# Scheduling the splits behind a rotation, and the split of the recurrence's input, behind the products traced ahead of them

## The chip, the cores and the metric

The kernel runs on one core of a Trainium2 chip. The metric is the device time of one execution in microseconds (us). Before the change it is 1851.07 us, the median of three runs (1850.51 to 1853.98). The execution that the profiler recorded took 1852.94 us; its span, from the first to the last instruction, is 1851.2 us, and 1.7 us lie around it.

## The reference

Two layers of a hybrid block on x of 512 tokens x 1024, all in fp32. Cut to what matters here:

```python
h = rms_norm(x, g_pre_mix);  proj = h @ w_in      # q k v qi ki wi xr gr zu zv gates
q, k, qi, ki = (apply_partial_rope(t) for t in (q, k, qi, ki))   # the rotation
score = einsum(wi, relu(qi . ki)) * idx_scale      # the indexer: 8 heads
sel = top_k(score, 128)                            # keys that each query may see
y_a = softmax(q . k on sel) @ v                    # 8 heads of attention
xr = causal_depthwise_conv(xr)
y_b = rg_lru(xr) * gelu(gr)                        # the recurrence
y_c = gelu(zu) * spatial_gating(rms_norm(gelu(zv)))
x = x + rms_norm((sum_n sigmoid(gate_n) * (y_n @ w_branch_n)) @ w_out)
x = x + rms_norm(relu(rms_norm(x) @ w_up)**2 @ w_dn)
x = x + rms_norm((p @ w_ple) * sigmoid(x @ w_gate))
```

## The kernel before, in words

Activations lie transposed in SBUF, 128 features by 512 tokens to a tile. To keep fp32 accuracy, each operand of a product is split in two fp32r halves, hi (a cast on ACT) and lo (a subtraction of hi, on DVE or POOL), and a product is three matmuls on PE: hi.hi, lo.hi, hi.lo (`mm3`, lines 298 to 300).

**Weights.** They come in tiles of 128x1024 in the order written out in `order`. `prep` (line 231) does one: a DMA on SP's queue into one of 3 buffers `wr`, the cast `wh` on ACT (line 243), the subtraction `wl` on DVE (line 244). There are 4 buffers for `wh` and `wl`, so the preparation of a tile waits until PE has finished the tile four places earlier. `getw` (line 247) fetches a tile and prepares up to three ahead. A tile of `w_in` is 24 matmuls of 512 columns (`proj`, through `gemm`).

**The order of the work.** A Python program traces the instructions; a planner in the framework then fixes, once and on estimated durations, the order of each engine's queue: of the instructions whose inputs it holds for ready it takes the one traced first. On the chip each engine takes its queue in that order. The trace itself is ordered by a clock of its own, `clk`: each step of a product advances it by its length in us (`tick`), and `defer(us, fn)` has `fn` traced when the clock has come that much further. `run_later(force=True)` traces all that is left at once. Generators (the indexer, attention, the recurrence) are advanced in the same way.

**The beginning of a layer.** `xr0` to `xr3` are projected while x arrives (`gemm_arriving`), in two halves of 256 tokens in the second layer; the norm's factors R come from `Stats.row`, whose `complete` defers a few small instructions (`rstd_tok`: products on PE at line 408, DVE at 427, POOL at 428; then a transposition on PE at 434 and a copy on ACT at 443). Then the convolution for `xr` on DVE (606 to 611), then `ki`, `qi0` to `qi3`. `rope` (line 570) is the rotation: DVE multiplies and shuffles the product (573, 574), POOL multiplies and adds (575, 576). Its result is split for the next products by `ki_split` (ACT 369, 628, 629, DVE 370), `stacked` (ACT 650 twice, DVE 651 twice) or `q_split` (ACT 1026 and 1028, DVE 1027), deferred by TURN = 5. `xc_split` (ACT 616, POOL 617) splits the convolution's output; only the recurrence's gates use it, much later. `wi_turn` transposes the indexer's weights on PE (639).

**Then** `tokens(1, ...)` (line 580) projects zv: four weight tiles ("chunks") for two token blocks at a time, 12 matmuls to a chunk in each of two passes (line 590), zu, the spatial gating, gr, the recurrence, and the gates and branches. The indexer (products at 667 to 671 or 681, scores on ACT 692 and DVE 695 to 699, then 96 rounds of max and replace on DVE at 714 and 716 in both layers) runs as a generator beside all of these and gives the mask BIAS (POOL 729, 730). It is forced to its end by `finish(idxq)` after the first q and k of attention. In attention, `logits` wait for Q and K; the softmax is DVE 939 and 941, ACT 940 and 942; `turn` transposes on PE (953) and splits on ACT 369 and DVE 370; `values` are products at 967.

Of the kernel before, what the change touches and what calls it, by code (L numbers as in the profile page):

```python
# [17 lines left out]
S = 512  # L18
# [27 lines left out]
def f32v(ap):  # L46
    return ap.bitcast(F32)
# [3 lines left out]
def hybrid_block_kernel(ctx, tc, xT, pT, pos, vec, bsp, freq, w_in, w_tok, w_lru, w_sp, w_br, w_out, w_up, w_dn, w_ple, w_gate, out, depth=DEPTH, dbg=None):  # L51
    nc = tc.nc
# [14 lines left out]
    def tmp(dt=F32):  # L67
        return tp.tile([128, S], dt, tag="tmp", name=nm("tmp"), bufs=NTMP)
# [4 lines left out]
    def bank():  # L73
        return pp.tile([128, 512], F32, tag="ps", name=nm("ps"), bufs=8)

    def slot(tag, dt=F32, big=False):
        return cp.tile([128, 4, S] if big else [128, S], dt, tag=tag, name=nm(tag))
# [10 lines left out]
    TAIL = 3  # L88
    LEAD = 256
    ATT = 13  # L90
    TURN = 5
    WARM = 120
    FIRST = [0, 1, 4]

# [152 lines left out]
    def getw(key, ahead=LA):  # L247
        assert order[nget[0]][0] == key, (order[nget[0]][0], key)
        nget[0] += 1
        while nprep[0] < min(nget[0] + ahead, len(order)):  # L250
            prep()
        return prepared.pop(key)
# [8 lines left out]
    def defer(us, fn):  # L261
        later.append((clk[0] + us, uid[0], fn))
        uid[0] += 1

    def run_later(force=False):
        while later:
            later.sort(key=lambda e: e[:2])
            if not force and later[0][0] > clk[0]:
                return
            later.pop(0)[2]()  # L270

    def add_task(q, gen):
        q["wait"].append(gen)
# [17 lines left out]
    def finish(q):  # L291
        run_later(force=True)
        while q["act"] or q["wait"]:
            tick(0.3)
# [7 lines left out]
    def gemm(ps, w, xs, kk, c0=0, st=None, r=FULL):  # L302

        h3, l3 = [v.rearrange("p (k c) -> p k c", k=kk) for v in w]
        for k in range(kk):
            if st is not None and k == kk - 2:
                st.partial()
            mm3(ps, h3[:, k, c0:c0 + 128], l3[:, k, c0:c0 + 128], xs[k][0][:, r], xs[k][1][:, r], k == 0, k == kk - 1)
            tick(0.65 * width(r) / S)
# [67 lines left out]
    class Stats:  # L377
# [59 lines left out]
        def row(self, div, dst):  # L437


            def complete(r):  # L440
                def tok():
                    self.rstd_tok(div, r)
                    defer(3.0, lambda: A.copy(dst[:, r], self.rstd_bc(r)))

                defer(2.2, tok)

            return complete

# [84 lines left out]
    for l in range(depth):  # L533
        vc = vecs[l]

        def col(c):
            return vc[:, c:c + 1]
# [18 lines left out]
        def proj(name, ahead=LA):  # L556
            ps = bank()
            gemm(ps, getw(("in", l, name), ahead), XS, KT)
            return ps
# [11 lines left out]
        def rope(ps, n=128):  # L571
            t1, u = tmp(), tmp()
            V.tensor_mul(t1[:n], ps[:n], Cr[:n])
            V.stream_shuffle(u[:n], ps[:n], mask=SHUF)
            G.tensor_mul(u[:n], u[:n], Sr[:n])  # L575
            G.tensor_add(t1[:n], t1[:n], u[:n])  # L576
            return t1
# [19 lines left out]
        idxq = {"wait": [], "act": [], "max": 1}  # L597
# [5 lines left out]
        for j in range(4):  # L603
            ps = first[j]
            xr = tmp()
            V.tensor_mul(xr, ps, R)
            xc = slot(f"M{4 + j}")
            A.activation(xc, xr, AF.Identity, bias=col(V_CB + j), scale=col(V_CW + 12 + j))
            for i in range(3):
                s = 3 - i  # L610
                V.scalar_tensor_tensor(xc[:, s:], xr[:, :S - s], col(V_CW + 4 * i + j), xc[:, s:], op0=ALU.mult, op1=ALU.add)
            xh, xl = slot(f"B{j}", F32R), slot(f"B{4 + j}", F32R)
            XC.append((xc, xh, xl))

            def xc_split(xc=xc, xh=xh, xl=xl):
                A.copy(xh, xc)
                G.tensor_sub(xl, xc, f32v(xh))

            defer(10 + 5 * j, xc_split)


        ps = proj("ki")
# [5 lines left out]
            A.copy(kih[64:128], kf[0:64])  # L628
            A.copy(kil[64:128], f32v(kil[0:64]))

        defer(TURN, ki_split)
        wf = tmp()
        A.copy(wf, ps)
        WI = small(32, "wi", 2).rearrange("p (t h) -> p t h", t=4)
# [5 lines left out]
            for t in range(1, 4):  # L640
                V.tensor_scalar(WI[:, t, :], pw[:, t * 128 + 64:t * 128 + 72], rt[:, t:t + 1], IDX_SCALE, op0=ALU.mult, op1=ALU.mult)

        defer(9, wi_turn)

        def stacked(f, q0, q1):


            for s, q in enumerate((q0, q1)):
                r, other = slice(64 * s, 64 * s + 64), slice(64 - 64 * s, 128 - 64 * s)
                A.copy(q[r], f[r])  # L650
                V.tensor_sub(q[other], f[r], f32v(q[r]))
            return q0, q1

        QI = []
        for j in range(4):
            ps = proj(f"qi{j}")
            QI.append((slot(f"A{j}", F32R), slot(f"A{4 + j}", F32R)))
            defer(TURN, lambda f=rope(ps), q=QI[j]: stacked(f, *q))

        def qk(a, b, c, d, jobs):  # L660

# [23 lines left out]
        def scores(t, sc):  # L685
            n = 128 * (t + 1)
            qs = slice(t * 128, (t + 1) * 128)
            for j in range(4):
                pr = qk_full(QI[j], kih, kil, t, n)
                for s in range(2):  # L690
                    rl = tmp()
                    A.activation(rl[:, :n], pr[s][:, :n], AF.Relu)
                    w = WI[:, t, 2 * j + s:2 * j + s + 1]
                    if j == 0 and s == 0:
                        V.tensor_scalar(sc[:, :n], rl[:, :n], w, None, op0=ALU.mult)
                    else:
                        V.scalar_tensor_tensor(sc[:, :n], rl[:, :n], w, sc[:, :n], op0=ALU.mult, op1=ALU.add)
                yield 3.4
            V.tensor_add(sc[:, qs], sc[:, qs], tri)

        def indexer():
            sc = {t: tmp() for t in (1, 2, 3)}
            for t in (1, 2, 3):
                yield from scores(t, sc[t])
            for t in (1, 2, 3):
                yield from select(t, sc[t])

        def select(t, sc):
            n = 128 * (t + 1)
            wk = tmp()  # L710
            m8 = None
            for r in range(TOPK // 8):
                m8 = small(8, "m8", 4)
                V.max(m8, (sc if r == 0 else wk)[:, :n])  # L714
                if r < TOPK // 8 - 1:
                    V.match_replace(wk[:, :n], m8, (sc if r == 0 else wk)[:, :n], -3.0e38)  # L716
                yield 0.8 + 1.1 * t
            thr = m8[:, 7:8]
            gt, cnt = tmp(), small(1, "cnt", 4)
            V.tensor_scalar(gt[:, :n], sc[:, :n], thr, None, op0=ALU.is_gt, op1=ALU.add, accum_out=cnt)  # L720
            rem = small(1, "cnt", 4)
            V.tensor_scalar(rem, cnt, -1.0, float(TOPK), op0=ALU.mult, op1=ALU.add)
            eq = tmp()
            V.tensor_scalar(eq[:, :n], sc[:, :n], thr, None, op0=ALU.is_equal)

            V.tensor_tensor_scan(wk[:, :n], eq[:, :n], eq[:, :n], 0.0, ALU.add, ALU.max)
            yield 2.0
            V.scalar_tensor_tensor(eq[:, :n], wk[:, :n], rem, eq[:, :n], op0=ALU.is_le, op1=ALU.mult)
            G.tensor_add(gt[:, :n], gt[:, :n], eq[:, :n])
            G.tensor_scalar(BIAS[t], gt[:, :n], -NEG, NEG, op0=ALU.mult, op1=ALU.add)  # L730
            yield 1.0

        defer(9, lambda: add_task(idxq, indexer()))


        bs = tmp()
# [23 lines left out]
        for j in range(4):  # L760
            ps = proj(f"zu{j}")
# [16 lines left out]
        for j in range(4):  # L778
# [3 lines left out]
            for hf in range(2):  # L782
                ps = bank()
# [4 lines left out]
                for s in range(2):  # L788
                    r = slice(64 * s, 64 * s + 64)
# [55 lines left out]
        for j in range(4):  # L845
# [7 lines left out]
            r, i = tmp(), tmp()  # L853
# [59 lines left out]
        KK = [slot("K0", F32R, True), slot("K1", F32R, True)]  # L913
# [105 lines left out]
        for j in range(4):  # L1019
            f = rope(proj(f"q{j}"))  # L1020
            q2, ql = (slot(f"A{j}", F32R), slot(f"A{4 + j}", F32R)), tmp(F32R)

            def q_split(f=f, q2=q2, ql=ql):
                for s in range(2):
                    r, other = slice(64 * s, 64 * s + 64), slice(64 - 64 * s, 128 - 64 * s)
                    A.copy(q2[s][r], f[r])
                    V.tensor_sub(ql[r], f[r], f32v(q2[s][r]))
                    A.copy(q2[s][other], f32v(q2[s][r]))

            defer(TURN, q_split)  # L1030
            Q.append((q2, ql))
            defer(TURN, lambda f=rope(proj(f"k{j}")), j=j: stacked(f, KK[0][:, j], KK[1][:, j]))
            if j == 0:
                finish(idxq)
            defer(ATT, lambda j=j: add_task(attq, attention(j)))
            gated(1, YB, ds=range(2 * j, 2 * j + 2))
# [23 lines left out]
        for d in range(5):  # L1060
            ps = bank()
# [8 lines left out]
        ps = bank()  # L1070
# [52 lines left out]
        for c in range(2):  # L1123
# [3 lines left out]
            for i in range(4):  # L1127
                ps = bank()
# [14 lines left out]
        for d in range(5):  # L1143
            if d < 4:
                ps = first[d]
            else:
                ps = bank()
# [95 lines left out]
```

## Time and profile before

| | |
|---|---|
| median of three runs | 1851.07 us (1850.51 to 1853.98) |
| the profiled execution | 1852.94 us |
| its span | 1851.2 us, 22873 instructions |
| PE busy | 1803.0 us (97%) |
| DVE busy | 1159.5 us (63%) |
| ACT busy | 800.3 us (43%) |
| POOL busy | 361.6 us (20%) |
| mean granted clock of TensorE | 0.990 |
| chain that ended last | PE 72%, DVE 12%, POOL 6%, issue 6%, ACT 4% |

A busy share says how long an engine had work in it, not that it ran at its peak. PE is busy almost throughout, so what can be won without fewer products is the idle time of PE, some 48 us, and the time in which its clock was granted at less than full. The view of waits says for each of these idle times which instruction ended it.

### The profile page before, as it was taken

The page shows a single profiled execution, that of the slowest core. Times are in us where ns is not written, and L with a number is a line of the kernel's source. Part 1 is how long each engine was busy: PE and PEld are TensorE (multiplying, and loading weights), DVE is VectorE, ACT ScalarE, POOL GpSimd, SP SyncE. Part 2 cuts the span into 40 slices and gives each one's busy share as a digit, 9 for nine tenths or more (in the row PEclk, how much of TensorE's full clock was granted, in tenths as well). Part 3 has the DMA queues.
Part 4 walks back from the last instruction along what each step waited for, and adds up shares of the span by engine and source line. Part 5 has one row for each costly group of instructions (what it writes and reads, how often), then busy time and mean ns, then how long its engine had stood idle before and what let it go on. Part 6 is the DMA issues. An engine that isn't in the chain of part 4 may idle for free.

```text
span 1851.2 us, 22873 instructions
## 1 busy us (share of the span) xinstructions
PE 1803.0 (97%) x8798; PEld 1507.5 (81%) x8798; DVE 1159.5 (63%) x1939; ACT 800.3 (43%) x1292; POOL 361.6 (20%) x292
## 2 busy tenths in 40 slices
PE   8899999999999999999998999999999999999997
PEld 7787887888888888888887878877888888888886
DVE  6689996666386253533685999866563852544355
ACT  5466435664453322223455573455544432222233
POOL 3513212210240000003454141222004200000033
PEclk9999999999999999999999999999999999999999
DMA  5122322222223232332212223222222222222321
GB/s 173 63 92 85 98 92 91 69 80 82 90 80 108 97 98 96 99 106 91 92 58 97 68 92 103 91 80 72 89 80 92 92 92 101 96 97 97 108 80 58
DMA packets 49678, 167.77 MB, mean 91 GB/s; under 512 B 6048, under 2 KB 8864, under 8 KB 49568
## 3 DMA queue, kind: packets, MB, share of 16 engines
q1 hardware_dynamic: 47376, 163.64, 26.8%
q10 hardware_dynamic: 2192, 2.67, 0.4%
q8 instruction: 69, 1.13, 0.3%
q14 instruction: 41, 0.34, 0.1%
HBM read 164.19 MB, written 2.10 MB: 90 GB/s over the span
## 4 chain that ended last, share of the span: by engine, by line
PE 72%; DVE 12%; POOL 6%; issue 6%; ACT 4%; DMA 0%; SPq 0%; POOLq 0%; DVEq 0%; ACTq 0%
PE ps L298 21%; PE ps L299 20%; PE ps L300 20%; PE ps L356 3%; PE ps L590 3%; DVE wl L244 2%; POOL tmp L575 1%; POOL tmp L576 1%; DVE tmp L716 1%; DVE m L714 1%; POOL sacc L398 1%; POOL X L483 1%; PE ps L681 1%; PE ps L967 1%; DVE tmp L790 1%
## 5 line engine op out<-in xcount | busy, mean ns | idle before, releaser
L243 ACT CAST wh<-wr 128x1024 fp32r<-128x1024 f32 x303 | 316.6, 1049 | 453.3 <-PE ps L300 365.9
L244 DVE TENSOR_TENSOR wl<-wr,wh 128x1024 fp32r<-128x1024 f32 x303 | 386.8, 1280 | 188.7 <-ACT wh L243 188.0
L298 PE MATMUL ps<-xh,wh 128*128 128x512 f32 (+1 forms) x1296 | 502.7, 388 | 0.9 <-DVE tmp L370 0.9
L299 PE MATMUL ps<-xh,wl 128*128 128x512 f32 (+1 forms) x1296 | 495.5, 382 | 3.0 <-DVE wl L244 3.0
L300 PE MATMUL ps<-xl,wh 128*128 128x512 f32 (+1 forms) x1296 | 495.6, 382 | 0.0
L398 POOL TENSOR_TENSOR sacc<-sacc,tmp 128x256 f32<-128x256 f32 (+1 forms) x99 | 109.8, 1109 | 894.8 <-issue 584.5
L300 PEld LDWEIGHTS ps<-xl,wh 128*128 128x128 f32 x1296 | 243.9, 188 | 48.2
L299 PEld LDWEIGHTS ps<-xh,wl 128*128 128x128 f32 x1296 | 244.4, 189 | 47.1 <-DVE wl L244 3.9
L298 PEld LDWEIGHTS ps<-xh,wh 128*128 128x128 f32 x1296 | 244.0, 188 | 47.2 <-issue 1.9
L300 PE MATMUL ps<-V,wh 128*128 128x512 f32 (+1 forms) x528 | 195.4, 370 | 0.0
L298 PE MATMUL ps<-K,wh 128*128 128x512 f32 (+1 forms) x432 | 158.2, 366 | 0.0
L299 PE MATMUL ps<-K,wl 128*128 128x512 f32 (+1 forms) x432 | 157.8, 365 | 0.0
L300 PE MATMUL ps<-B,wh 128*128 128x512 f32 x336 | 130.9, 390 | 0.0
L298 PE MATMUL ps<-A,wh 128*128 128x512 f32 x320 | 125.0, 391 | 0.2 <-ACT A L369 0.2
L299 PE MATMUL ps<-A,wl 128*128 128x512 f32 x320 | 124.6, 389 | 0.0
L1102 DVE TENSOR_TENSOR M<-M,ps 128x512 f32<-128x512 f32 x48 | 33.0, 688 | 141.4 <-PE ps L300 141.4
L300 PEld LDWEIGHTS ps<-V,wh 128*128 128x128 f32 x528 | 99.5, 188 | 16.7
L1090 DVE TENSOR_TENSOR tmp<-ps,R 128x512 f32<-128x512 f32 x64 | 43.8, 690 | 108.6 <-PE ps L300 108.5
L356 PE MATMUL ps<-xl,wh 128*128 128x256 f32 (+1 forms) x264 | 88.1, 334 | 6.2 <-DVE xl L503 5.5
L298 PEld LDWEIGHTS ps<-K,wh 128*128 128x128 f32 x432 | 81.5, 189 | 13.3
L299 PEld LDWEIGHTS ps<-K,wl 128*128 128x128 f32 x432 | 81.5, 189 | 13.1
L356 PE MATMUL ps<-xh,wh 128*128 128x256 f32 (+1 forms) x264 | 87.1, 330 | 2.2 <-ACT xh L493 2.2
(237 smaller groups left out, 2733.0 us busy)
## 6 DMA issues: line engine op xcount, KB each, us to landing
wr<-in_w_in_dram SPq DMA_DIRECT2D x95, 512.0 KB, 3.3
wr<-in_w_up_dram SPq DMA_DIRECT2D x64, 512.0 KB, 3.3
wr<-in_w_dn_dram SPq DMA_DIRECT2D x64, 512.0 KB, 3.3
wr<-in_w_br_dram SPq DMA_DIRECT2D x24, 512.0 KB, 3.3
wr<-in_w_tok_dram SPq DMA_DIRECT2D x16, 512.0 KB, 3.3
wr<-in_w_out_dram SPq DMA_DIRECT2D x16, 512.0 KB, 3.3
wr<-in_w_gate_dram SPq DMA_DIRECT2D x16, 512.0 KB, 3.3
X<-in_xT_dram SPq DMA_DIRECT2D x8, 256.0 KB, 5.9
```

Of the source, the lines that this page charges most:

```text
L243: A.copy(hi, raw)
L244: V.tensor_sub(lo, raw, f32v(hi))
L298: PE.matmul(ps, wh, xh, start=start, stop=False)
L299: PE.matmul(ps, wl, xh, start=False, stop=False)
L300: PE.matmul(ps, wh, xl, start=False, stop=stop)
L356: PE.matmul(pss[o][:, r], (h3, l3, h3)[m][:, q], xs[q][m // 2][:, r], start=q == 0 and m == 0, stop=q == KT - 1 and m == 2)
L398: G.tensor_add(sacc[:, r], sacc[:, r], self.q[r.start, r.stop])
L483: (G if d in on_g else V).tensor_add(X[d][:, r], X[d][:, r], ys[d][:, r])
L575: G.tensor_mul(u[:n], u[:n], Sr[:n])
L590: PE.matmul(ps, x, w, start=k == 0 and i == 0, stop=k == KT - 1 and i == 2)
L1090: V.tensor_mul(t, ps, R)
L1102: V.tensor_add(F[d], F[d], ps)
```

## The change

A helper `behind_products(fn)` traces what `fn` traces, and gives each of its instructions on ACT, DVE and POOL an edge to the last PE instruction traced so far. The edge is for the planner alone (no semaphore, nothing on the chip): it may not place the instruction before that product. `turn_later` defers such a call. The splits after a rotation and `xc_split` go through it. TURN goes from 5 to 7, `xc_split` from 10 + 5j to 12 + 5j, `wi_turn` from 9 to 14, the indexer's start from 9 to 12. In `Stats.row`, the first half's `tok` is deferred by 8.0 in place of 2.2; where there are no halves, and for the second half, it stays at 2.2.

```diff
-    TURN = 5
+    TURN = 7
+    def behind_products(fn):
+        ins = nc.cur_bb.bb.instructions
+        n0 = len(ins)
+        mark = next(i for i in reversed(ins[:n0]) if i.engine == mybir.EngineType.PE)
+        fn()
+        for i in nc.cur_bb.bb.instructions[n0:]:
+            if i.engine in (mybir.EngineType.Activation, mybir.EngineType.DVE, mybir.EngineType.Pool):
+                tc.add_manual_dep(i, mark.name, mybir.DependencyInfo(mybir.DependencyClass.NoSync, mybir.DependencyReason.SCHED_ONLY), reason="behind products")
+    def turn_later(us, fn):
+        defer(us, lambda: behind_products(fn))
...
-                defer(2.2, tok)
+                defer(2.2 if r.stop == S else 8.0, tok)
...
-            defer(10 + 5 * j, xc_split)
+            turn_later(12 + 5 * j, xc_split)
...
-        defer(TURN, ki_split)
+        turn_later(TURN, ki_split)
...
-        defer(9, wi_turn)
+        defer(14, wi_turn)
...
-            defer(TURN, lambda f=rope(ps), q=QI[j]: stacked(f, *q))
+            turn_later(TURN, lambda f=rope(ps), q=QI[j]: stacked(f, *q))
...
-        defer(9, lambda: add_task(idxq, indexer()))
+        defer(12, lambda: add_task(idxq, indexer()))
...
-            defer(TURN, q_split)
+            turn_later(TURN, q_split)
...
-            defer(TURN, lambda f=rope(proj(f"k{j}")), j=j: stacked(f, KK[0][:, j], KK[1][:, j]))
+            turn_later(TURN, lambda f=rope(proj(f"k{j}")), j=j: stacked(f, KK[0][:, j], KK[1][:, j]))
```

## Rows read from the trace of the kernel before

**Rows 1.** Waits of PE, whole execution: who <- whom: us in total, times, longest.
```profile
PE ps L590 <- DVE wl L244: 10.5, 4, 4.2
...
PE ps L299 <- DVE wl L244: 4.4, 4, 1.5
PE ps L967 <- ACT tmp L369: 4.1, 4, 2.3
PE ps L434 <- POOL rt L428: 2.5, 3, 1.7
...
PE ps L967 <- DVE tmp L370: 1.7, 4, 0.9
...
PE ps L639 <- ACT tmp L633: 1.2, 2, 0.7
```

**Rows 2.** Stretches: length, busy us (x instructions) PE PEld DVE ACT POOL, clock, DMA.
```profile
75.25:79.46 4.21, 0.00 (x1) 0.01 (x1) 3.98 (x4) 2.50 (x5) 2.27 (x2) 0.74 0.04 17
79.46:83.90 4.44, 4.44 (x11) 3.51 (x12) 3.79 (x6) 0.50 (x1) 1.61 (x1) 0.50 0.49 161
...
994.18:998.60 4.42, 4.42 (x10) 3.46 (x11) 3.80 (x6) 0.50 (x1) 1.58 (x1) 0.50 0.56 170
...
540.00:900.00 360.00, 360.00 (x1600) 298.05 (x1599) 174.35 (x210) 111.19 (x139) 21.05 (x14) 1.00 0.30 99
```

**Rows 3.** ACT in order of time: start, us, instruction [idle before <- releaser].
```profile
60.70 0.62 ACT L369 CAST M<-tmp 64x512 fp32r<-64x512 f32 x1 [5.60 <-POOL tmp L576]
...
63.28 1.06 ACT L243 CAST wh<-wr 128x1024 fp32r<-128x1024 f32 x1
68.21 1.26 ACT L650 CAST A<-tmp 64x512 fp32r<-64x512 f32 x2 [3.87 <-POOL tmp L576]
69.49 1.05 ACT L243 CAST wh<-wr 128x1024 fp32r<-128x1024 f32 x1
74.73 1.26 ACT L650 CAST A<-tmp 64x512 fp32r<-64x512 f32 x2 [4.18 <-POOL tmp L576]
```

**Rows 4.** DVE in order of time, the same stretch.
```profile
70.96 1.23 DVE L244 TENSOR_TENSOR wl<-wr,wh 128x1024 fp32r<-128x1024 f32 x1
...
75.38 2.76 DVE L651 TENSOR_TENSOR A<-tmp,A 64x512 fp32r<-64x512 f32 x2 [1.93 <-ACT A L650]
78.18 1.23 DVE L244 TENSOR_TENSOR wl<-wr,wh 128x1024 fp32r<-128x1024 f32 x1
```

**Rows 5.** POOL in order of time, the same stretch.
```profile
53.95 4.11 POOL L617 TENSOR_TENSOR B<-M,B 128x512 fp32r<-128x512 f32 x1 [1.34 <-ACT B L616]
...
65.53 1.29 POOL L575 TENSOR_TENSOR tmp<-tmp,tmp 128x512 f32<-128x512 f32 x1
...
71.00 2.33 POOL L575 TENSOR_TENSOR tmp<-tmp,tmp 128x512 f32<-128x512 f32 x1 [2.83 <-DVE tmp L574]
```

**Rows 6.** Line 650, whole execution: ACT's idle time before it (us, times) until:
```profile
  POOL tmp L576: 58.6, 16
```

**Rows 7.** Attention of the second layer: ACT in order of time.
```profile
1209.32 1.26 ACT L1026 CAST A<-tmp 64x512 fp32r<-64x512 f32 x2 [5.73 <-POOL tmp L576]
...
1211.76 0.47 ACT L369 CAST tmp<-ps 128x384 fp32r<-128x384 f32 x1
```

**Rows 8.** The same place as a stretch, columns as in Rows 2.
```profile
1212.28:1217.40 5.12, 4.97 (x17) 3.99 (x18) 4.87 (x8) 1.51 (x2) 0.63 (x1) 0.67 0.19 53
```

**Rows 9.** A stretch of the gates and branches, columns as in Rows 2.
```profile
200.00:220.00 20.00, 19.34 (x86) 15.69 (x85) 19.73 (x35) 6.16 (x9) 1.29 (x1) 1.00 0.33 106
```

**Rows 10.** DVE in order of time, just after that stretch.
```profile
219.49 1.21 DVE L244 TENSOR_TENSOR wl<-wr,wh 128x1024 fp32r<-128x1024 f32 x1
```

**Rows 11.** PE in order of time, the first use of that tile.
```profile
221.13 0.39 PE L299 MATMUL ps<-xh,wl 128*128 128x512 f32 x1
```

**Rows 12.** The first softmax of the first layer: ACT, in order of time.
```profile
287.21 0.72 ACT L942 ACTIVATE tmp<-tmp,mx 128x512 f32<-128x512 f32 x1
```

**Rows 13.** PE in order of time, the transposition that reads it.
```profile
287.82 0.60 PE L953 MATMUL ps<-ident,tmp 128*128 128x128 f32 x4
```

## The prediction, made before the changed kernel ran

> **What bounds the kernel now.** I read the waits of PE first, since PE is busy 97% of the span and only its idle time and its clock can be won here. The reader is to see in them that the longest wait which is no start-up of a stage is that of the zv projection (line 590) for a `wl` that DVE makes: 10.5 us in four times, up to 4.2 at once [rows 1]. Then I took stretches around it: from 75.25 to 79.46 PE does nothing at all, and for the next 4.44 us its granted clock is 0.50, the lower level (1.2 GHz), so the wait is paid a second time [rows 2]. The second layer shows the same behind its own wait, 994.18 to 998.60 [rows 2].
>
> Why is that `wl` late? ACT and DVE in order of time answer it. DVE makes the subtraction at 78.18 right behind two of line 651, which had waited for line 650 on ACT [rows 4], and ACT had stood 4.18 us until POOL's rotation was done; the casts of weights at 63.28 and 69.49 likewise come right behind splits that had kept ACT idle for 5.60 and 3.87 us [rows 3]. So an engine with little to do (ACT is idle in most of these rows) is held at the head of its queue by a split whose input POOL has not finished, and the weight behind it, whose raw data and buffer are there, is late. Over the execution ACT lost 58.6 us in 16 such places before line 650 alone [rows 6]. In attention it is the same with line 1026: 5.73 us idle, and only after it the cast (line 369) for which PE's `values` stand 2.3 us [rows 1, 7].
>
> **The change, part by part.** No instruction is added or removed: the edges are for the planner, so there is no new semaphore and no new wait; queues are reordered. I cost each part by the wait it can end. The unit of PE: 1600 matmuls in 360 us, 0.225 each [rows 2], so 12 products of a chunk take 2.7 us and a tile of 24 takes 5.4.
>
> A, *the splits of ki and qi, and `xc_split`, in the zv projection.* Each projection advances the trace's clock by 5.2 (8 steps of 0.65). With TURN = 5 a split was traced in the last step of the next projection, just ahead of the `getw` that prepares a weight; with 7 and the edge it comes some 2 us into the projection after that, so the planner has the cast (1.05) and the subtraction (1.23) of the weight ahead of it [rows 3, 4]: 2.3 us against 2 us and the split's own cast of 0.6. The weights of chunks 1 to 4 so stand in front of the splits that held them. What goes: 10.5 us of waits [rows 1] and the slow clock behind two of them. In 79.46 to 83.90 PE starts 11 products in 4.44 us, for which 2.5 would do: 1.9 lost; in 994.18 to 998.60 it starts 10 in 4.42: 2.2 lost [rows 2]. Together 14.6 us. What is late next: the fourth chunk. Its cast stands behind the second `stacked`, whose rotation POOL finishes only after the two ahead of it and `xc_split`s of up to 4.11 us [rows 5]; a rest of 0.5 us a layer seems likely to me. Bounds: 0 (the weights stay late) to 14.6; I take 13.6, near the upper end, because the rows show no other cause of this wait. `xc_split`, 0.6 on ACT and 4.11 on POOL at worst [rows 5], has only the recurrence's gates waiting for it, some 70 us on; moving it back also lets POOL begin ki's rotation earlier. The DMAs of weights on SP's queue wait for `wr` buffers that `wl` frees, so they move earlier; those of the gating's bias, on ACT's queue, change places with splits and are read after zv.
>
> B, *`wi_turn` from 9 to 14.* PE's transpositions waited 1.2 us in two times for a copy on ACT [rows 1], itself behind `xc_split`s. Five us later the copy is done. 0 to 1.2; I take 1.2. Its three small DVE operations are needed by the indexer only, which starts later still.
>
> C, *the splits of q and k in attention.* The waits of `values` are 4.1 and 1.7 [rows 1]; behind the longest the mean clock is 0.67 over 5.12 us [rows 8], that is 3.4 us at half clock, 1.7 lost. Together 7.5. The split of q(j+1) was traced 5 after its projection, and the planner put it ahead of `turn`'s cast, which [rows 7] then waited for the rotation. Two us later and behind the products it should come after that cast in most rounds. Against it: `logits` of the next round need these splits, and come 13 after k; instead of 8, 6 us are left for 2.7 us of ACT and DVE work. Bounds: -3 (that margin is missed by 0.4 us in each of 8 rounds) to 7.5; I take 5.5, as waits on DVE (1.7) have other work of DVE ahead of them.
>
> D, *the first half's row, 2.2 to 8.0.* Of three waits of line 434 for `rt`, 2.5 us, the one of 1.7 belongs to the last norm, which is not touched [rows 1]; 0.8 is left, in the up projections. The step moves behind the last products of the second half; PE then meets the last `xl` instead, so I take half, 0.4 (0 to 0.8). R as a whole is complete only with its second half, which stays.
>
> E, *the indexer from 9 to 12.* It starts 3 us later against PE's work. In the stretch of gates DVE is busy 19.73 of 20 us [rows 9], so the mask comes up to 3 us later. That costs nothing while the first softmax of attention is ahead of PE; it just is: the last normalisation ends where the transposition of it begins, 287.9 [rows 12, 13]. On the other hand q's split no longer holds DVE there. Bounds 0 to 6 for both layers; I take 1.0.
>
> Sum: 13.6 + 1.2 + 5.5 + 0.4 - 1.0 = 19.7 us. The profiled execution took 1852.94, so 1833.2 for one like it; the median of the runs is 1.9 lower, and from it the forecast is 1831.4 us.
>
> *A rule against it.* POOL's multiplication of a rotation took 1.29 us alone and 2.33 where DVE's `wl` subtraction began beside it [rows 4, 5]. Suppose all POOL work from ki's rotation on met such a subtraction: three rotations of 2 x 2.33 and two `xc_split`s of 4.11 are 22.2 us; from 53.95, where POOL is seen to take up an `xc_split` [rows 5], that is 76.2, and with split, cast and subtraction (1.26, 1.05, 1.23) the fourth chunk is ready at 79.7. The third was wanted at 75.25 after an earlier wait of (10.5 - 2 x 4.2) / 2 = 1.05 [rows 1, 2], so the fourth would be at 74.2 + 2.7 = 76.9. That is 2.8 us of wait and some 2 for the clock behind it, 9.6 in both layers: 10.1 us of gain are left, 1841. The Trainium skill (SBUF — State Buffer, "Who interferes with whom") says that a VectorE instruction with two SBUF inputs and a GpSimd instruction that reads SBUF exclude one another for as long as the first of them lasts. By that rule such meetings are certain once the subtractions stand closer to the rotations; the trace agrees in the pair above (2.33 against 1.29). I keep it a rival, since 1.29 stands in the rows too and not every operation can meet one.
>
> **The rivals.** (1) *Given back to DVE.* In the gates DVE is full [rows 9], and a tile's subtraction ended at 220.70, 0.43 us ahead of its first use [rows 10, 11]; four waits of 4.4 us are there already [rows 1]. If PE comes 7 us earlier and DVE cannot, A is lost again in small waits: 1851.1 - 1.2 - 5.5 - 0.4 + 1.0 = 1845.0. Against it: DVE stood idle in the zv stretch for the same splits [rows 4], and moves forward with PE. (2) *POOL's rotation stays the bound*, as worked out above: 1841. (3) *Not what it says.* The estimated order comes out as before, because on the planner's durations POOL was never late; then only B and D are left: 1851.1 - 1.6 = 1849.5. For it speaks that the old order, too, was made by that planner; against it that the edge bars the old place. (4) *Slower: the mask.* DVE alone sets the mask's time, PE reaches the first softmax 7.3 us a layer earlier (A) and the indexer starts 3 later; PE then waits 10.3 for a softmax that is just in time today [rows 12, 13] and runs 2 us at the low clock: -7.3 + 10.3 + 2.0 = +5 a layer, +10, less B and D, with C at nothing: 1859.5. It decides from the point at which DVE has no idle time left between 100 and 260 us.
>
> **How the numbers follow.** The forecast has 0.57, given back to DVE 0.15, POOL 0.09, no effect 0.10, slower 0.09. Range: the forecast's own best is every upper bound at once (24.1) and some of line 299's waits (4.4) [rows 1], 1823; upward it takes in rivals 2 and 1 with a rest, 1846. Within 0.2% (3.7 us) is what a measurement of this kernel cannot tell from no change. Faster by more than that: 0.57 + 0.15 + 0.09 = 0.81; within: 0.10; slower: 0.09.
>
> **What would show it.** In the waits of PE after the change, line 590 for `wl` should be under 1.5 us in total (A), line 639 gone (B), `values` under 3 (C), line 434 near 1.8 (D); no stretch at clock 0.50 in the zv projections; ACT's idle time before line 650 well below 58.6, with casts of weights ahead of each split. Line 299's waits above 12 would be rival 1, a wait for the fourth chunk behind POOL rival 2, the same order on ACT rival 3, a wait of line 953 for the softmax rival 4. If ACT's idle time falls and line 590's wait stays, the chain I read is wrong.

## The result, and the profile after

The changed kernel takes 1838.97 us (median of four runs, 1835.20 to 1840.58) where the kernel before took 1850.85 in the same comparison: a ratio of 0.9929, 95% interval 0.9911 to 0.9948, or 11.9 us less. The forecast was 1831.4, with a range of 1823 to 1846. The direction and the range held; of the 19.7 us of the sum, 7.8 did not come.

The profiled execution of the changed kernel is its fastest, 1835.2 us with a span of 1833.5, so the two profiles differ by 17.7 us and not by 11.9. Lines of the code stand 14 or 15 higher than before: 299 is now 313, 356 is 370, 428 is 442, 434 is 448, 503 is 518, 590 is 605, 650 is 665, 967 is 982. First the page of the changed kernel (busy time of the engines, and the shares of the chain that ended last):

```profile
PE 1796.5 (98%) x8798; PEld 1504.8 (82%) x8798; DVE 1171.4 (64%) x1939; ACT 794.7 (43%) x1288; POOL 369.0 (20%) x292
...
PE 80%; DVE 9%; POOL 5%; issue 3%; ACT 3%; DMA 0%; SPq 0%; ACTq 0%; POOLq 0%; DVEq 0%
```

Then its waits of PE, in the columns of [rows 1]:

```profile
PE ps L313 <- DVE wl L244: 9.4, 5, 3.3
PE ps L370 <- DVE xl L518: 5.4, 10, 1.1
PE ps L605 <- DVE wl L244: 3.9, 2, 2.0
...
PE ps L448 <- POOL rt L442: 1.7, 1, 1.7
```

The zv projection's wait of 10.5 us in four times is 3.9 in two, those of `values` and `wi_turn` are gone, line 434's 2.5 is 1.7. Against that the row of line 299 (now 313) in [rows 1], which the prediction counted only in its best case and in rival 1, has more than doubled: products wait 9.4 us for `wl` where they waited 4.4.

ACT stands less at the head of its queue. The 58.6 us of [rows 6] are 31.2 ahead of the splits of qi and 27.4 ahead of those of attention's k (who <- whom: us, times, longest):

```profile
ACT A L650 <- POOL tmp L576: 31.2, 8, 5.9
...
ACT K L650 <- POOL tmp L576: 27.4, 8, 5.7
```

In the changed kernel, where line 650 is 665, the second row is gone and the first is left:

```profile
ACT A L665 <- POOL tmp L591: 18.5, 6, 4.6
```

Stretches of the changed kernel, columns as in [rows 2]: the 4.45 us behind the wait that is left in zv, the 5.72 and 4.71 us behind the two longest waits of line 313, and 177 us with the first layer's attention.

```profile
74.95:79.40 4.45, 4.45 (x19) 3.67 (x20) 4.28 (x3) 1.58 (x3) 4.37 (x3) 1.00 0.36 118
179.77:185.49 5.72, 5.72 (x14) 4.46 (x15) 5.36 (x9) 4.40 (x6) 4.56 (x3) 0.50 0.28 93
1087.29:1092.00 4.71, 4.71 (x15) 3.79 (x16) 4.39 (x7) 4.41 (x6) 3.55 (x3) 0.68 0.33 111
...
268.00:445.00 177.00, 176.76 (x877) 144.91 (x876) 120.27 (x238) 102.21 (x209) 33.23 (x22) 1.00 0.25 84
```

The same places in the kernel before:

```profile
268.00:445.00 177.00, 173.05 (x852) 140.39 (x851) 115.34 (x233) 101.11 (x207) 34.52 (x24) 1.00 0.24 78
...
179.24:184.00 4.76, 4.76 (x21) 3.95 (x22) 4.76 (x4) 3.63 (x5) 4.76 (x3) 1.00 0.73 220
```

The granted clock of 0.50 (1.2 GHz), which stood behind zv's wait in [rows 2], now stands behind the wait of 3.3 us at 179.77: 14 products in 5.72 us. Behind the wait of 1.5 us that the kernel before had in this part of its code, at 179.24, the clock stayed at 1.00 and 21 products started in 4.76. In the 177 us PE starts 877 products where it started 852; since attention begins and ends earlier after the change, the last 10 of these us are no longer attention's, and the table below is the better measure.

To see every stretch at once I add up from the trace, over consecutive instructions of PE, the time from start to start beyond the median of that shape in the trace of before (0.227 us for 512 columns). This holds idle time and slow clock together, in us:

| stretch | before | change | edges only | times only | indexer at 9 | before, indexer 12 | attention alone | xc late |
|---|---|---|---|---|---|---|---|---|
| first 50 us, start-up | 7.6 | 4.8 | 6.5 | 6.6 | 6.5 | 7.9 | 7.5 | 5.7 |
| ki, qi, zv, layer 1 | 8.9 | 2.4 | 8.4 | 9.5 | 3.9 | 9.5 | 9.4 | 0.5 |
| gr, recurrence, gates, layer 1 | 2.8 | 7.8 | 2.8 | 7.8 | 2.8 | 7.8 | 2.8 | 2.9 |
| attention, layer 1 | 9.3 | 3.6 | 5.2 | 6.7 | 3.6 | 7.9 | 3.6 | 3.6 |
| up projections, both layers | 2.2 | 2.8 | 2.2 | 2.8 | 2.8 | 2.2 | 2.2 | 2.8 |
| norm, ki, qi, zv, layer 2 | 16.4 | 9.6 | 14.4 | 17.0 | 11.2 | 16.6 | 15.8 | 7.8 |
| gr, recurrence, gates, layer 2 | 2.8 | 7.9 | 2.8 | 7.8 | 2.8 | 7.8 | 2.8 | 2.9 |
| attention, layer 2 | 9.6 | 3.2 | 3.6 | 6.3 | 4.3 | 8.2 | 4.3 | 4.3 |

(The last six columns are experiments below.) From before to the change: zv and what lies around it gain 6.5 + 6.8 = 13.3, attention 5.7 + 6.4 = 12.1; the gates lose 5.0 + 5.1 = 10.1, the up projections 0.6. That is 14.7 us, with 2.8 from the start-up 17.5 of the 17.7 that the two executions differ. I don't count the start-up as an effect of the change: it is 4.8 to 7.9 in these eight profiles, and follows no edit.

### The profile page after: what moved, and what is told of

It is laid out like the page before. It is cut to its first block, busy times and chain, and to the rows that moved or that the text cites. A ratio compares the mean times of both kernels' runs of the same rounds, so it can differ in the third digit from the quotient of the medians.

```text
span 1833.5 us, 22875 instructions
## 1 busy us (share of the span) xinstructions
PE 1796.5 (98%) x8798; PEld 1504.8 (82%) x8798; DVE 1171.4 (64%) x1939; ACT 794.7 (43%) x1288; POOL 369.0 (20%) x292
## 4 chain that ended last, share of the span: by engine, by line
PE 80%; DVE 9%; POOL 5%; issue 3%; ACT 3%; DMA 0%; SPq 0%; ACTq 0%; POOLq 0%; DVEq 0%
PE ps L312 23%; PE ps L314 23%; PE ps L313 23%; PE ps L605 4%; PE ps L370 3%; DVE wl L244 1%; PE ps L982 1%; DVE tmp L731 1%; PE ps L968 1%; POOL X L498 1%; DVE m L729 1%; PE ps L696 1%; POOL sacc L412 1%; POOL tmp L590 1%; DVE M L626 1%
```

## The experiments

Each median stands beside its ratio to the kernel before, which ran on the same chip.

**1. Attention's splits as before the change.**

```diff
-            turn_later(TURN, q_split)
+            defer(5, q_split)
...
-            turn_later(TURN, lambda f=rope(proj(f"k{j}")), j=j: stacked(f, KK[0][:, j], KK[1][:, j]))
+            defer(5, lambda f=rope(proj(f"k{j}")), j=j: stacked(f, KK[0][:, j], KK[1][:, j]))
```

> The changed kernel with attention's splits of q and k as they were (deferred by 5, no edge); all the rest of the change stays. Theory: attention's part of the gain (C) was larger than the prediction's 5.5 us: the waits of `values` and the slow clock behind them add to about 8.4 us in the trace of before. Then this kernel takes 1839.0 + 8.4 = 1847.4 us, and its waits of PE show `values` for `tmp` again, about 5.8 us. Rival 1: C is the 5.5 of the prediction: 1844.5. Rival 2: the gain came from the zv stretch alone and attention's waits were hidden elsewhere: 1839.0, within 2 us of the change.

1845.97 us (0.9977, 0.9968 to 0.9986): 7.0 slower than the change, between the theory and the first rival. The waits of `values` came back, but as 3.9 us (2.1 and 1.8) and not 5.8.

**2. The edges alone; 3. the times alone.** In 2 all times are those of before the change and only `turn_later` stays; in 3 the times are the new ones and `turn_later` is `defer` again.

> The edges to the products alone: every time of tracing as before the change (TURN 5, 10 + 5j, 9, 9, the row at 2.2), the splits through the new helper. Theory: what moved the splits behind the weights is the later tracing, and the edge only bars a place a little earlier than that; line 590's wait for `wl` stays near 10 us, and the time is between 1846 and 1851. Rival: the edge alone carries the effect, since the planner may not place the split before the product: 1839 to 1842, with line 590's wait under 4 us.

> The later times of the change without the edges (TURN 7, 12 + 5j, 14, 12, the row at 8.0, plain deferral). Theory: the later tracing carries most of the effect, and the edge is worth only the cases in which a split still slips in ahead of a weight (the third `stacked` of the zv stretch, some of attention): 1840 to 1844 us. Line 590's waits are then those of the fourth chunk and a little longer than the 3.9 us of the change. Rival: without the edge the splits go back to the head of the queue: 1848 to 1851.

2 took 1839.19 us (0.9939, 0.9927 to 0.9951) and 3 took 1857.66 (1.0038, 1.0026 to 1.0050). Both theories missed the time: the later times alone make the kernel slower than before, and the edges alone reach the whole change's time. The theory for the edges was right on zv, whose wait stays near 10 us; its rival had the time, but by a gain in zv that did not come. Waits of PE, edges alone:

```profile
PE ps L605 <- DVE wl L244: 10.8, 2, 5.7
...
PE ps L313 <- DVE wl L244: 4.3, 4, 1.5
```

Times alone:

```profile
PE ps L313 <- DVE wl L244: 10.4, 6, 3.2
PE ps L605 <- ACT wh L243: 8.0, 4, 2.6
...
PE ps L605 <- DVE wl L244: 3.6, 4, 1.5
```

The edges alone cure attention (18.9 us to 8.8 in the table) and leave zv's wait at 10.8. The times alone leave zv at 8.0 + 3.6, now for the cast, since a split still slips in ahead of it on ACT; they give attention half its gain, and bring the loss in the gates. So zv needs the edge and a later time, attention the edge, and something among the times costs 10 us. Which of the times zv needs (TURN, `xc_split`'s or `wi_turn`'s) was not taken apart.

**4. The indexer's start back at 9, in the changed kernel.**

```diff
-        defer(12, lambda: add_task(idxq, indexer()))
+        defer(9, lambda: add_task(idxq, indexer()))
```

> The changed kernel with the indexer's start back at 9. Theory: the stretch of the recurrence's gates lost about 9 us against before (waits of line 299 for `wl` from 4.4 to 9.4, and two stretches at a lower granted clock behind them) because PE comes 8 us earlier to work of DVE and POOL that did not move forward, and the later indexer adds its 3 us a layer to that. Starting it at 9 again moves that work forward by at most 3 us of the 3.3 of each long wait: 1833 to 1836 us, if the work on DVE there is a queue of fixed length. Rival: it is the recurrence and not the indexer that holds the queue there, and the start is without effect: 1838 to 1840. Other rival: the earlier scores take back DVE and ACT time from the zv stretch: 1841 or more.

1830.14 us (0.9891, 0.9878 to 0.9904): 8.8 us faster than the change, better than the theory's best, and without any loss in the gates although PE comes there earlier than in any kernel so far. Waits of PE:

```profile
PE ps L313 <- DVE wl L244: 4.4, 4, 1.6
PE ps L605 <- DVE wl L244: 3.9, 2, 2.0
```

Line 313 is back at the 4.4 of [rows 1]. Its waits are also at the products of before: that at 173.10 is for the weight which the kernel before waited for at 179.24, two weight tiles ahead of the one that the change waits for at 179.77. When PE comes to that later one (181.39) its `wl` is long there (176.16, against 179.72 in the change). The theory's reason, a queue of DVE that only moves by 3 us, doesn't explain such a swap.

**5. The indexer's start at 12, in the kernel before.** The same edit the other way round, with nothing else of the change.

> The kernel before with one edit, the indexer's start from 9 to 12. Theory: the 9 us that the change lost in the stretch of the recurrence's gates come from this edit alone, by the order it gives DVE's queue there (a `wl` then stands behind four multiplications of the recurrence that wait for POOL), whenever PE gets there. Then it loses as much here, where the zv waits are still in place and PE is late: 1850.7 + 9 = 1860 us (1857 to 1862), with waits of line 299 for `wl` near 9 to 10 us in place of 4.4. Rival 1 of the prediction (PE comes earlier, DVE cannot): no loss here, since PE is not earlier: 1849 to 1852. Third: the mask of the first softmax is late (the term E of the prediction): a wait of line 953 or 967 near 290 us, with line 299 as it was.

1859.44 us (1.0038, 1.0026 to 1.0051), 7.4 slower than before in that comparison. PE is 10 us later there than in the changed kernel, and the loss in the gates is the same 5.0 in both layers, with the long wait at the same product (189.95) as in the change. Without the edit the kernel before has the `wl` for it at 182.30 and PE comes to it at 187.53; with the edit it is ready at 189.90. Waits of PE:

```profile
PE ps L299 <- DVE wl L244: 10.4, 6, 3.3
```

Line 590's wait is the 10.5 of [rows 1] still, so the loss is no gain of zv given back. DVE in order of time, before with the indexer at 12 (start, us, instruction, idle before and its releaser; some rows between are left out):

```profile
173.70 1.48 DVE L244 TENSOR_TENSOR wl<-wr,wh 128x1024 fp32r<-128x1024 f32 x1 [2.44 <-ACT wh L243]
...
177.43 1.77 DVE L869 SCALAR_TENSOR_TENSOR B<-tmp,B 128x512 f32<-128x512 f32 x1 [2.25 <-POOL tmp L868]
...
188.68 1.22 DVE L244 TENSOR_TENSOR wl<-wr,wh 128x1024 fp32r<-128x1024 f32 x1
```

The changed kernel, same view:

```profile
163.51 1.49 DVE L244 TENSOR_TENSOR wl<-wr,wh 128x1024 fp32r<-128x1024 f32 x1 [2.44 <-ACT wh L243]
167.25 1.77 DVE L884 SCALAR_TENSOR_TENSOR B<-tmp,B 128x512 f32<-128x512 f32 x1 [2.25 <-POOL tmp L883]
...
170.92 1.52 DVE L884 SCALAR_TENSOR_TENSOR B<-tmp,B 128x512 f32<-128x512 f32 x1
...
173.49 1.66 DVE L884 SCALAR_TENSOR_TENSOR B<-tmp,B 128x512 f32<-128x512 f32 x1
...
175.54 0.67 DVE L884 SCALAR_TENSOR_TENSOR B<-tmp,B 128x512 f32<-128x512 f32 x1
...
178.51 1.21 DVE L244 TENSOR_TENSOR wl<-wr,wh 128x1024 fp32r<-128x1024 f32 x1
```

The two idle times in brackets are equal to the hundredth in both kernels, and the rows lie 10.2 us apart. The `wl` at 178.51, whose cast ACT had finished at 172.34, stands behind all four multiplications of the recurrence (line 884), rounds of the selection and the two idle times, 4.69 us in which DVE's queue waited for ACT and POOL. With the indexer at 9 in the changed kernel (same view) two of the four are ahead of the weights, and three subtractions follow in a row:

```profile
167.17 1.76 DVE L884 SCALAR_TENSOR_TENSOR B<-tmp,B 128x512 f32<-128x512 f32 x1 [1.22 <-POOL tmp L883]
...
171.23 0.68 DVE L884 SCALAR_TENSOR_TENSOR B<-tmp,B 128x512 f32<-128x512 f32 x1
171.83 4.34 DVE L244 TENSOR_TENSOR wl<-wr,wh 128x1024 fp32r<-128x1024 f32 x3
```

The kernel before, where the start is 9 too, has the same order, again with two multiplications ahead of three subtractions:

```profile
177.97 4.33 DVE L244 TENSOR_TENSOR wl<-wr,wh 128x1024 fp32r<-128x1024 f32 x3
```

So with the start at 9 all three weights stand behind two of the recurrence's multiplications, and PE waits 1.5 us for the first; with 12 the first stands ahead of all four, the third behind all four, and PE waits 3.3 us for the third. The Trainium skill (PSUM — Partial Sum Buffer, "Engine vs sequencer instructions") says that the queues of ScalarE, VectorE and GpSimd are strictly first in, first out. The changed kernel's rows agree: a ready subtraction waited 6.2 us behind what the planner had put ahead of it.

**6. Attention's splits alone, in the kernel before** (edge and 7 us; zv, indexer and row as before).

> The kernel before with the edge and the time 7 for attention's splits of q and k alone; the zv stretch, the indexer and the row as before. Theory: attention's part is worth what the change lost when it was taken out, 1846.0 - 1839.0 = 7.0, up to the 8.4 of its waits and slow clock in the trace: 1850.7 - 7.7 = 1843.0 (1842 to 1844), and no wait of `values` for `tmp` above 0.3 us. Rival (the prediction's size): 5.5, 1845.2. Rival: it works only together with the rest: 1848 or more.

1840.68 us (0.9938, 0.9925 to 0.9950): 11.4 us faster, more than the theory's 7.7 and twice the prediction's 5.5; `values` no longer wait. Attention falls from 9.3 and 9.6 to 3.6 and 4.3 in the table; zv's 10.5 and line 313's 4.4 stay. Taken out of the change (experiment 1) it was worth 7.0, since the other edits alone had lowered attention from 18.9 to 15.8 in the trace.

**7. `xc_split` later, with the indexer at 9.**

```diff
-            turn_later(12 + 5 * j, xc_split)
+            turn_later(34 + 5 * j, xc_split)
```

> The changed kernel with the indexer at 9 and with `xc_split` traced at 34 + 5j in place of 12 + 5j, so that POOL has only the rotations while the zv weights are prepared. Theory: what is left of line 605's wait (2.0 us in each layer, with slow clock behind it of about 1) is the fourth chunk, late because POOL and DVE slow each other while rotation, `xc_split` and the subtractions meet; without `xc_split` there POOL's rotations start earlier and the wait goes: 1830.1 - 4 to 6 = 1824 to 1826 us. Rival: the rotations of qi2 and qi3 alone are enough to hold DVE; the wait stays at 1 to 2 us: 1829 to 1831. Other rival: `xc_split` meets zu and the spatial gating and takes time there: 1831 or more.

1823.86 us (0.9851, 0.9838 to 0.9865), 6.3 less than experiment 4 and 28.2 below the kernel before. Waits of PE:

```profile
PE ps L313 <- DVE wl L244: 4.5, 4, 1.6
...
PE ps L605 <- DVE wl L244: 0.2, 1, 0.2
```

Line 605 is done with. How: DVE in order of time in the second layer, indexer at 9 (experiment 4), first the split of ki, then the `wl` of the third chunk and that of the fourth, for which PE waits:

```profile
964.52 1.11 DVE L384 TENSOR_TENSOR M<-tmp,M 64x512 fp32r<-64x512 f32 x1 [3.08 <-ACT M L383]
...
973.09 1.81 DVE L244 TENSOR_TENSOR wl<-wr,wh 128x1024 fp32r<-128x1024 f32 x1
...
979.56 1.21 DVE L244 TENSOR_TENSOR wl<-wr,wh 128x1024 fp32r<-128x1024 f32 x1
```

and the same with `xc_split` late:

```profile
959.16 1.11 DVE L384 TENSOR_TENSOR M<-tmp,M 64x512 fp32r<-64x512 f32 x1 [1.83 <-ACT M L383]
...
967.73 1.21 DVE L244 TENSOR_TENSOR wl<-wr,wh 128x1024 fp32r<-128x1024 f32 x1
...
973.61 1.21 DVE L244 TENSOR_TENSOR wl<-wr,wh 128x1024 fp32r<-128x1024 f32 x1
```

POOL at the rotation of ki, experiment 4 (an `xc_split`, line 632, then the rotation's second half), then with `xc_split` late:

```profile
960.19 2.40 POOL L632 TENSOR_TENSOR B<-M,B 128x512 fp32r<-128x512 f32 x1
962.55 1.28 POOL L591 TENSOR_TENSOR tmp<-tmp,tmp 64x512 f32<-64x512 f32 x1
```

```profile
956.19 2.29 POOL L591 TENSOR_TENSOR tmp<-tmp,tmp 64x512 f32<-64x512 f32 x1
```

From the split of ki to the fourth `wl` DVE has no idle time in either run, so a delay at the start of this stretch arrives at its end. An `xc_split` of 2.40 us stood between the two halves of ki's rotation; without it DVE stands 1.83 us for ki's split in place of 3.08, which is 1.25 us. The third chunk's subtraction takes 1.21 where it took 1.81 behind an `xc_split` that had begun before it, which is 0.60. Together 1.85, and PE's wait falls from 2.0 us to 0.2. So two thirds were the place in POOL's queue, and one third the mutual slowing that the expectation named. The first layer shows the same (3.08 and 1.84, 1.81 and 1.20).

**8. The recurrence 8 us later, indexer at 12.** A `yield 8.0` ahead of the recurrence's first loop.

> The changed kernel, indexer at 12 as in the change, with the recurrence started 8 us later against the products (a first `yield 8.0`). Theory: the wait for `wl` at 179.77 in the change is that of a subtraction queued on DVE behind the recurrence's four multiplications, each of which waits for POOL's square and runs at 1.5 to 1.8 us beside it; with the recurrence later, that `wl` stands ahead of them and the long waits (3.3 us in each layer) and the slow clock behind them go: 1839.0 - 9 = 1830 (1829 to 1833). Rival: it is the selection's rounds that fill DVE there, and the loss stays: 1837 to 1840. Other rival: the wait moves with the recurrence to the next weights: line 313's waits for `wl` again near 9 us, 1837 to 1842.

1841.15 us (0.9939, 0.9926 to 0.9953). The wait at 179.77 went and two came back at 197.96 (3.4 us) and 218.22 (2.0), as the second rival had it; the gates lose 18.7 us where the change loses 15.6:

```profile
PE ps L313 <- DVE wl L244: 10.9, 4, 3.4
```

**9. The recurrence's square on DVE, indexer at 12.**

```diff
-                G.tensor_mul(q, a, a)
+                V.tensor_mul(q, a, a)
```

> The changed kernel, indexer at 12 as in the change, with the recurrence's square `q = a * a` on DVE in place of POOL; nothing else. Theory: the `wl` that PE waits for at 179.77 is late because DVE stands at the recurrence's multiplications for POOL's squares (2.25 us idle before the first) and runs them at 1.5 to 1.8 us beside POOL in place of 0.67. With the square on DVE there are four more instructions of about 0.6 us, but no wait and no POOL beside them: 2.25 + 3 x 0.95 = 5.1 us saved, 2.4 paid, so the `wl` comes some 2.7 us earlier and the long wait shrinks from 3.3 to about 0.6 us, with the slow clock behind it gone: 1839.0 - 2 x (2.7 + 1.5) = 1830.6 (1829 to 1834). Rival: DVE is simply full there, and four more instructions on it make the wait longer: 1840 to 1843. Other rival: the wait moves on to the next weight of the stretch: 1836 to 1839.

1833.57 us (0.9896, 0.9879 to 0.9912): 5.4 less than the change (against the kernel before on the same chip, 0.9896 where the change has 0.9929), with four more instructions a layer on the engine that seemed full. Waits of PE:

```profile
PE ps L312 <- ACT wh L243: 3.7, 2, 1.8
PE ps L313 <- DVE wl L244: 2.2, 4, 0.8
```

The wait of 3.3 us is 0.3, near the theory's 0.6; a part moved on, to 195.41, where PE waits 1.8 for a cast. DVE in order of time:

```profile
166.76 1.72 DVE L884 SCALAR_TENSOR_TENSOR B<-tmp,B 128x512 f32<-128x512 f32 x1
...
170.15 0.68 DVE L884 SCALAR_TENSOR_TENSOR B<-tmp,B 128x512 f32<-128x512 f32 x1
...
171.82 1.68 DVE L884 SCALAR_TENSOR_TENSOR B<-tmp,B 128x512 f32<-128x512 f32 x1
...
175.75 1.21 DVE L244 TENSOR_TENSOR wl<-wr,wh 128x1024 fp32r<-128x1024 f32 x1
```

POOL in the same stretch:

```profile
166.65 1.29 POOL L871 TENSOR_TENSOR M<-M,tmp 128x512 f32<-128x512 f32 x1
171.65 1.29 POOL L892 TENSOR_TENSOR B<-B,M 128x512 f32<-128x512 f32 x1 [3.71 <-ACT B L889]
```

The `wl` comes 2.8 us earlier than in the change, but the theory's sum is not what happened. Two multiplications take 0.68 us (170.15, and 175.15, not shown), and two still take 1.72 and 1.68, beside multiplications of POOL that are no squares. The Trainium skill (SBUF — State Buffer, "Who interferes with whom") says that a VectorE instruction with two SBUF inputs contends with a GpSimd instruction that reads SBUF. These rows agree: the two with work of POOL beside them are the long ones. What is gone are the 2.25 us of waiting for POOL, some 0.9 of the slowing, and two rounds of the selection (some 2 us), which stand ahead of this `wl` in the change and behind it here; against that stand 3.3 us for the four squares. The run shows that the edit helps, not which of these three did it.

**10 to 12: three tries on the kernel of experiment 7**: the indexer's start at 6; the square on DVE; the recurrence 8 us later.

> The kernel with the indexer at 9 and `xc_split` at 34 + 5j (1823.9), with the indexer's start at 6. Theory: the time of the start acts through the place of the selection's steps in DVE's queue, not through its amount; in the order that 6 gives, the selection is further on when the recurrence starts, two `wl` stand directly behind the recurrence's first two multiplications and the third behind the other two. The first waits (1.6 us in each layer) shrink and a new one for the third weight of up to 2 us can come: 1821 to 1827. Rival (the amount counts): 3 us less of DVE's work is ahead in each layer and all four waits for `wl` there go: 1823.9 - 5 = 1819. Other rival: the scores, 3 us earlier, meet the zv weights on ACT and DVE, and line 605's wait comes back: 1827 or more.

> The kernel with the indexer at 9 and `xc_split` at 34 + 5j (1823.9), with the recurrence's square on DVE in place of POOL. Theory: three `wl` stand behind the recurrence's first two multiplications in DVE's queue; without the wait for POOL's squares (1.2 us) and without POOL beside them (1.76 against 0.67), less 1.2 us for two squares, they come about 1.1 us earlier, and the wait of 1.6 us of each layer shrinks to about 0.5: 1823.9 - 2.2 = 1821.7 (1820 to 1823). Rival: DVE is full: 1825 to 1827.

> The kernel with the indexer at 9 and `xc_split` at 34 + 5j (1823.9), with the recurrence 8 us later. Theory after the run of the later recurrence in the changed kernel, where the waits moved on to the next weights (3.4 and 2.0 us): the same happens here; the first wait (1.6 us) goes, and waits of line 313 come back 15 to 30 us later in sum of 2 to 5 us in each layer: 1824 to 1834. Rival: with the selection further on there is room for the recurrence, and the waits of line 313 go: 1819 to 1821.

10 took 1829.75 us (0.9879, 0.9862 to 0.9896), 11 took 1824.19 (0.9846, 0.9832 to 0.9861), 12 took 1823.95 (0.9847, 0.9832 to 0.9862). The theory for 10 missed (1821 to 1827); its second rival had the time, but line 605 does not wait. With the start at 6 the waits for `wl` of the gates are back:

```profile
PE ps L313 <- DVE wl L244: 9.5, 4, 2.8
```

The gates lose 15.6 us in both layers together at 12 (experiment 5), 5.7 at 9 (experiment 4; 5.8 with `xc_split` late), and 15.6 again at 6 (`xc_split` late). It is not an amount of work that comes too early or too late; each start gives another order. 11 and 12 cannot be told from 7: 11 lies 1.2 us above its theory's range, 12 at the lower edge of its own. In 11 line 313's waits fell from 4.5 us to 2.9, and in 12 the two waits of each layer became one of 2.0; neither shows in the time.

## Why the prediction was right or wrong

**A, zv.** The mechanism held: the splits moved behind the weights, ACT's idle time ahead of those of qi fell from 31.2 to 18.5, and no stretch of zv is at clock 0.50. With B it gave 13.3 us in the trace where 14.8 was taken. What was mis-sized is the rest of the fourth chunk: "0.5 us a layer" was 1.9 and 2.0. Rival 2 named its place, `xc_split` and the rotations in POOL's queue, at 2.8 a layer, by slowing at every meeting; experiment 7 shows the place, with 1.25 us a layer for the queue and 0.60 for the slowing. "With 7 and the edge" is borne out: neither alone frees zv (experiments 2 and 3).

**B, `wi_turn`.** Gone, as taken. But it is gone in experiment 2 too, where `wi_turn` stays at 9 and only the edges are new, so the later time was not needed for it.

**C, attention.** Right cause, wrong size: 5.5 taken, at most 7.5; measured 11.4 alone, 7.0 as the last part of the change, 12.1 in the trace. I had counted the rows of `values` (5.8) and one slow stretch (1.7). Left out was line 298's wait of 0.9 for a subtraction of the same line 370, and what a stop costs beyond its row: in the trace of before a wait in attention costs 0.11 to 0.17 us more than its idle time (1.31 for 1.15 idle), nine times. A row counts idle time from the end of the product before, and a product of 512 columns ends 0.39 us after its start where the next one else starts after 0.23. The remaining 2 to 3 us I did not take apart. The feared wait of `logits` did not come.

**D, the row.** 0.4 taken, 0.6 lost in the trace: line 448 no longer waits there, and PE waits 0.5 us a layer for an `xl` in place of those 0.4. The four profiles in the table with 8.0 have 2.8 us in that stretch, the four with 2.2 have 2.2; a difference too small for the times to show, and no run has this edit alone.

**E, the indexer.** This step failed: 1.0 taken, 0 to 6 bounded, 10.1 in the trace, 7.4 to 8.8 in the times (experiments 5 and 4). I priced the delay at the end of the chain ("the mask comes up to 3 us later"), and there it did cost nothing. I did not price the queue in between: a generator that starts 3 us later gives every step of the selection another place on DVE among weights and the recurrence. "It starts 3 us later against PE's work" was true and was not the cost.

**The rivals.** Rival 1 had the place of the loss and something of its size (13.6 us in both layers, where 10.1 were lost), but its mechanism is refuted: experiment 5 has the loss without the earlier PE, experiment 4 the earlier PE without the loss. That the waits stood at 9.4 and not "above 12" was the hint. Rival 2 was real, at 3.9 us of waits; rivals 3 and 4 did not happen. That the time is no further off than 7.8 us is luck: in the trace E came out 9.1 us worse, A 1.5 and D 1.0, and C 6.6 better. With C at its 5.5 the time would have been some 1845 us, at the range's upper edge. (These make 5.0 of the 7.8; the rest lies between the profiled executions and the medians.)

## What to carry to other kernels

A step that is moved in a planned order must be priced at every in-order queue that it passes, not only where its result is used: 3 us of delay cost 9, by way of weights that depend on nothing that was delayed. When a change bundles edges and times, run each edit both ways, alone on the kernel before and undone in the kernel after: here that turned a gain of 11.9 us into one of 20.6 with one number put back, and, with one more moved (`xc_split` off the rotations' queue), into 28.2. An engine that looks full may be waiting at the head of its queue; giving it more work of its own, in place of a wait for another engine, made the kernel faster (experiment 9); with the indexer at 9 and `xc_split` late the same edit won nothing (experiment 11).

## What the runs showed of the hardware that was not expected

The granted clock behind a stop does not go by its length alone. After the waits of 3.3 us at 179.77 and 1087.29 the mean granted clock was 0.50 and 0.68 in the stretches shown above; after one of 1.5 us (179.24 before the change) it was 1.00. After zv's remaining wait of 1.9 us it was 1.00 in the changed kernel's profile (74.95:79.40), and 0.61 in the profile with the indexer at 9, behind the same wait:

```profile
76.66:81.00 4.34, 4.34 (x14) 3.63 (x15) 4.17 (x3) 1.49 (x3) 4.26 (x3) 0.61 0.34 121
```

So equal waits of 1.9 us cost 1.5 us more in one execution than in the other (2.4 and 3.9 us in the table's row). That may be a part of why the runs of one kernel spread over 5 us; it was not tried.
